# Weight differences ahead of their second parts, and four smaller changes of order, in a hybrid trunk kernel

## The chip, the cores and the metric

The kernel runs on one core of one Trainium2 chip. The metric is the device time of one execution in microseconds (us). In the profile TensorE is PE (its weight loads are PEld), VectorE is DVE, ScalarE is ACT, GpSimd is POOL and SyncE is SP. SP computes nothing; it issues transfers. An engine works through its instructions in program order, and so does a queue of transfers at its issuing end: an instruction that waits holds up all that stands behind it on that engine.

## The reference, cut to what matters

One layer of a streaming encoder over 2048 prompt frames and 32 sample frames of 1024 features, in float32.

```python
def layer(h, p, conv_hist, pool_hist, pos, g_mix, w_in, conv_w, conv_b, pool_w, pool_scale,
          w_out, g_ple, w_ple_gate, w_ple):
    hn = rmsnorm(h, g_mix)
    proj = hn @ w_in                                   # 1024 -> 3072
    hA, bA, cA, zA, vB, zB = jnp.split(proj, [W_A, 2 * W_A, 3 * W_A, 4 * W_A, 4 * W_A + W_B], axis=-1)
    yA, new_conv = short_conv_mixer(hA, bA, cA, zA, conv_hist, conv_w, conv_b)
    yB, new_pool = pooling_mixer(vB, zB, pool_hist, pos, pool_w, pool_scale)
    h = h + jnp.concatenate([yA, yB], axis=-1) @ w_out # 1024 -> 1024
    gate = jax.nn.sigmoid(rmsnorm(h, g_ple) @ w_ple_gate)
    h = h + (p @ w_ple) * gate                         # the embedding, 256 -> 1024
    return h, new_conv, new_pool
```

The first mixer is `b * conv3(c * h) * silu(z)`, a causal convolution of width 3 for each channel. The second takes trailing means over 2, 4, 8 and 16 frames less the frame itself, a 128x128 map for each group of channels, a scale, and times `silu(z)`. A last RMSNorm with `g_final` closes the trunk.

## The kernel before, in words

**Products in parts.** Every float32 operand of a matmul is held as two parts: a first part, cast to the type in which TensorE reads float32 at its full rate (a ScalarE copy, called cast in the profile), and a second part, the operand less the first (a VectorE subtraction). A product is then three matmuls for each 128 rows of the contraction: first by first, first by second, second by first (`FINE`, L100). `split` (L81 and L84) does this for frames and for the input projection's weights, `weight_part` (L195, L199, L202) for the weights of the later products.

**Seven products instead of eight.** Both operands are cut into 2 x 2 blocks and combined in the manner of Strassen. The weights come as 11, 21, 22 and the combinations T1 to T4 (one VectorE subtraction each, L195, which overwrites a block in place), the frames as 11, 12, 22 and S1 to S4. `seven` (L254) walks through the seven products with three PSUM banks X, Y, Z (x_o, y_o, z_o in the profile) and calls between them the functions that it is handed: `between` holds work to be issued after a product. `carry` and `out` take a finished bank to SBUF.

**Stages, in order of time.**

1. The input projection, up to about 536 us. Two groups of two tiles of 512 frames; for each of four channel blocks j three pairs of projections run, (zb, v), (c, h) and (za, b), each pair one `seven` of its own (`Unit`, L625 for its matmuls). With `both`, which is true for j = 0 of the second group only, the first two pairs run interleaved and the third follows. `pair_weights` prepares the weights of a pair; its `make(q)` makes the parts of one of them. `conv` (L1080) and `pool_sums`, `pool_split`, `mix` (L1062, L1072, L849 to L853) are the two mixers' own steps, placed between products by the table `mixes`. Beside the products of the first group, frames of the second are transposed on TensorE and combined (`four`, L465): a bank `pt_g` is taken, four transposes write it, VectorE or ScalarE reads it. `tbank` is a ring of two PSUM banks, `bank` one of six.
2. The embedding product (`embed`, L109) for the first seven tiles of 128 frames, 536 to 555 us. Its outputs lie in a space `eouts` and GpSimd's queue stores them (L168). The space belongs to a slot in which the weights 22 and T4 of the output product are put afterwards.
3. The output product with w_out, 555 to 726 us (`seven("o...")`, L185), pairs of tiles. T2 of its weights is made beside the last two embedding tiles; T3, then 21 and 22, then T4 beside the products of the first pair (`LATER`, where a number is the product behind which its function is called). `pin=True` keeps an instruction in the order in which it is written; the others may be put elsewhere by the scheduler. The lower rows of w_out, wo_b, are loaded on SP's queue, the last of them on GpSimd's.
4. The embedding for the remaining tiles, 726 to 754 us. Its weight wq is loaded on SP's queue (L1479) into a slot that the output product's last reads set free. The lower rows of the gate's weight, wg_b (L1363), and the frames' parts, pps (L129), are on the same queue.
5. The gate product, 754 to 930 us (`seven("g...")`), a loop over pairs of tiles, and a last pair with an order of its own (`last_pair`). For a pair the loop loads h and the embedding e (L377), and hn, the rows that are turned for the next pair; `gate_ops` adds to h (L1544), `done_g` squares, scales (GpSimd's ms_f and rstd_f, L73 and L77; VectorE's L1551) and stores (L1552, on GpSimd's queue). h's buffers are a ring, so that a load of h waits for the store of the tile that had the buffer before.

The weights' steps of the output product, cut from the code:

```python
        def third():
            hold.append(weight_parts(W, tops, bots, "T3", pin=True))

        def left():
            weight_parts(W, tops, bots, "21", pin=True)
            weight_slot(W, "wo", "22", "T4")
            hold.append(weight_parts(W, tops, bots, "22", pin=True))
            more(0)

        LATER = {1: third, 2: left, 3: later(1), 4: later("T4", 2)}
```

Of the kernel before, what the change touches and what calls it, by code (L numbers as in the profile page):

```python
# [9 lines left out]
F32 = mybir.dt.float32  # L10
F32R = mybir.dt.float32r
AF = mybir.ActivationFunctionType
ALU = mybir.AluOpType
# [16 lines left out]
NH = D // 2  # L30
KH = KC // 2
# [5 lines left out]
def trunk(ctx, tc, x_p, x_s, c_conv, c_pool, p_p, p_s, g_mix, w_in, conv_w, conv_b, pool_w,  # L37
          pool_scale, w_out, g_ple, w_gate, w_ple, g_fin, y_p, y_s, sc_p, sp_p, sc_s, sp_s):
    nc = tc.nc
# [6 lines left out]
    h_d = tc.dram_tile([T, D], F32, name="h_d")  # L46
# [140 lines left out]

    def weight_part(W, q, k, top, bot, ready=False, pin=False):

        b11, b12 = top[:, :NH], top[:, NH:]  # L190
        b21, b22 = (bot[:, :NH], bot[:, NH:]) if bot is not None else (None, None)
        t, x, y = {"11": (b11, None, None), "T1": (b11, b12, b11), "T2": (b11, b22, b11), "T3": (b12, b22, b12),
                   "22": (b22, None, None), "21": (b21, None, None), "T4": (b21, b21, b11)}[q]
        if x is not None and not ready:
            ins = nc.vector.tensor_tensor(t, x, y, op=ALU.subtract)  # L195
            if pin:
                tc.keep_in_program_order(ins)
        hi, lo = W[q][0][:, k], W[q][1][:, k]
        ins = nc.scalar.copy(hi, t)  # L199
        if pin:  # L200
            tc.keep_in_program_order(ins)
        return nc.vector.tensor_tensor(lo, t, hi.bitcast(F32), op=ALU.subtract)  # L202

    def weight_parts(W, tops, bots, *names, order=range(KH), pin=False):

        for q in names:
            for k in order:
                ins = weight_part(W, q, k, tops[k], bots[k] if bots else None, pin=pin)
        return ins
# [170 lines left out]
    with ExitStack() as s1:  # L380
# [20 lines left out]
        def put(piece, src, later=False):  # L401

            split(piece[:, :, 0], piece[:, :, 1], src, later=later)
# [56 lines left out]
        def turn(x, half, name, get=tbank, later=False):  # L460
            xt, n, _ = x
            pt = get(name)
            for k in range(KH):
                kk = half * KH + k
                ins = nc.tensor.transpose(pt[:, k * P:k * P + n], xt[:n, kk * P:(kk + 1) * P], ident[:n, :n])  # L465
                if later:
                    tc.keep_in_program_order(ins)
            return pt.rearrange("p (k t) -> p k t", k=KH)[:, :, :n]
# [5 lines left out]
        def four(xs, tag):  # L474

            for half in range(2):
                yield [turn(x, half, f"pt_{tag}_{i}_{half}", later=True) for i, x in enumerate(xs)]

# [99 lines left out]
        def pair_weights(gi, ka, kb, j, name, ring, s_ring, ring_b, pin):  # L578
# [31 lines left out]
            def make(q):  # L610
                if q == "S2":
                    sub(a11, s_t, a11)
                if q == "S4":
                    sub(a12, a12, a11)
                t = wtile(f"w_{name}_{q}")
                put(t, src[q])
                return t

# [52 lines left out]
        def in_turn(ins):  # L671
            tc.keep_in_program_order(ins)
# [142 lines left out]
        class Unit:  # L815
# [157 lines left out]
            def seven(self, B, aside, both=False):  # L973
# [20 lines left out]
                def h_first(ps):  # L994
                    mul(at(U, HU, 0), ps, self.cols(c_s, 0))
                    for b in range(2):
                        self.conv(b)

# [30 lines left out]

                def mix_and_split():  # L1030
                    self.mix(0)
                    self.pool_split(1)

                mixes = {(1, 2): first_mix, (1, 7): lambda: self.mix(1)}
                if both:
                    mixes = {(1, 7): lambda: self.pool_sums(1), (2, 2): mix_and_split, (2, 5): lambda: self.mix(1)}
                steps = [self.pair(*pairs[i], ring[i], ftile if both and i == 1 else None, both and i == 2) for i in range(3)]
# [239 lines left out]
    with ExitStack() as s2:  # L1277
# [142 lines left out]
        def third():  # L1420
            hold.append(weight_parts(W, tops, bots, "T3", pin=True))

# [52 lines left out]
        got = {0: load_pps(st.tile([P, 2, 2, P], F32R, tag="t", name=f"pps_{EARLY}"), EARLY, nc.sync)}  # L1475
        head, _ = rows_of_weight(cmb, "wg_b", g_d, 1, (0, 1))
        for k in range(2):
            for h in range(2):
                last_q = nc.sync.dma_start(wp[k][h].bitcast(F32), wl_d[k][h])  # L1479
        bots = head  # L1480
        with tc.issue_after(last_q.ins):
            bots += rows_of_weight(cmb, "wg_b", g_d, 1, (2, 3))[0]
        first_h = load_rows(xh, "hn", 0, h_d)
# [88 lines left out]
        def last_pair(i, A, before):  # L1572
# [9 lines left out]

            h = [load_rows(xh, "h", i + b, h_d) for b in range(2)]
            tt = nc.vector.tensor_tensor
# [167 lines left out]
        for k in range(KH):  # L1752
            weight_part(W, "T4", k, tops[k], bots[k], True)

# [12 lines left out]
        for i in range(0, NT - 3, 2):  # L1767
            A = S.pop(i)
            following = prep_g(i + 2, not i)
            h = [load_rows(xh, "h", i + b, h_d, queue=nc.sync if i else nc.gpsimd) for b in range(2)]  # L1770
            e = [load_rows(ya, "e", i + b, e_d) for b in range(2)]
            seven(f"g{i}", A, W, *gate_ops(h, e, P, f"g{i}", i), following)
            done_g(i, h[0])
            if i in (0, 2, 4):
                next(short_steps)
            if i + 2 < NT - 3:
                done_g(i + 1, h[1])
# [29 lines left out]
```

## Time and profile before

| what | us |
|---|---|
| median of 3 runs | 936.03 (935.65 to 938.8) |
| the profiled execution | 940.35 |
| its span | 938.3 |
| TensorE busy in the span | 909.1 |
| VectorE, ScalarE, GpSimd busy | 698.1, 459.0, 149.7 |
| mean granted TensorE clock | 0.991 of full speed |

The profile is of one execution. Its span runs from the first instruction to the last; the time of the execution includes what lies around it, 2.05 us here. A row of the timeline reads: start, duration, engine, line, operation, output and inputs by their names in the program, shape, count, and in brackets the idle time of the engine just before with what ended it. A row of the waits reads: who waited for whom, us in total, times, longest. A row of the windows gives the length of a stretch, busy us and instructions of each engine, the granted TensorE clock, the share of the transfer engines and the GB/s that they moved. A row of the transfers ends with the size and the us from issue to landing. In the chain that ended last each piece has a start and a length.

### The profile page before, as it was taken

Reading aid. Unit: us, or ns where it says so; the run is one execution under the profiler, and the core shown is the slowest. Engines: PE = TensorE matmul, PEld = TensorE weight load, DVE = VectorE, ACT = ScalarE, POOL = GpSimd, SP = SyncE. Lnnn points to the kernel's source line nnn. Section 1 sums busy time; section 2 is a strip of 40 time slices with the busy share of each in tenths; the row PEclk is TensorE's granted clock in tenths of the full one; section 3 lists DMA queues with packets and bytes.
Section 4 is the critical chain, followed back from the end, with each engine's and each line's share of the span. In section 5 each row is a group of like instructions: output and inputs, shape, how many; then the busy total and the mean of one; then the engine's idle time right before and its main releaser. Section 6 shows DMA issues by size and latency. Waiting matters only on the chain.

```text
span 938.3 us, 12210 instructions
## 1 busy us (share of the span) xinstructions
PE 909.1 (97%) x4186; PEld 727.1 (77%) x4186; DVE 698.1 (74%) x1148; ACT 459.0 (49%) x828; POOL 149.7 (16%) x295
## 2 busy tenths in 40 slices
PE   8999999999999999999999998999999999999996
PEld 6788887878888788766688885878787788778885
DVE  6895788797993787736668578765655988698884
ACT  7752544465453354523343375434434865456653
POOL 2200121222121032100010121112111211111112
PEclk9999999999999999999999998999999999999999
DMA  8165295747599674777753785776778776465653
GB/s 270 50 204 183 87 277 175 214 156 238 172 344 425 152 246 152 245 224 224 233 164 108 249 290 181 222 242 222 213 233 273 297 259 191 157 208 203 215 188 124
DMA packets 113243, 199.56 MB, mean 213 GB/s; under 512 B 13206, under 2 KB 69950, under 8 KB 112157
## 3 DMA queue, kind: packets, MB, share of 16 engines
q1 hardware_dynamic: 90749, 124.53, 42.3%
q0 software_dynamic: 19984, 69.87, 22.0%
q10 hardware_dynamic: 2448, 4.39, 1.3%
q8 instruction: 33, 0.54, 0.2%
q14 instruction: 29, 0.24, 0.1%
HBM read 133.06 MB, written 65.67 MB: 212 GB/s over the span
## 4 chain that ended last, share of the span: by engine, by line
PE 64%; DVE 5%; DMA 5%; ACT 2%; issue 2%; POOL 1%; POOLq 0%; SPq 0%; DVEq 0%; ACTq 0%
PE x_g L185 8%; PE x_zab L625 7%; PE x_o L185 6%; PE x_ch L625 6%; PE x_zbv L625 5%; PE e L109 4%; PE z_g L185 4%; PE z_zab L625 4%; PE z_ch L625 3%; PE z_o L185 3%; PE z_zbv L625 2%; PE y_g L185 2%; PE y_zab L625 1%; PE y_o L185 1%; PE new L1124 1%
## 5 line engine op out<-in xcount | busy, mean ns | idle before, releaser
L185 PE MATMUL x_o<-wo,y 128*128 128x512 f32 x192 | 48.3, 407 | 3.1 <-ACT wo L199 3.1
L185 PE MATMUL z_g<-wg,g_S 128*128 128x512 f32 x192 | 49.3, 401 | 0.0
L185 PE MATMUL x_o<-wo_T,y_S 128*128 128x512 f32 x192 | 47.5, 393 | 1.4 <-ACT wo_T L199 0.5
L185 PE MATMUL z_o<-wo,y_S 128*128 128x512 f32 x192 | 47.7, 390 | 0.5 <-ACT y_S L81 0.4
L185 PEld LDWEIGHTS x_o<-wo,y 128*128 128x128 f32 x192 | 38.0, 199 | 11.9 <-ACT wo L199 3.5
L185 PEld LDWEIGHTS x_o<-wo_T,y_S 128*128 128x128 f32 x192 | 35.6, 188 | 10.9 <-DVE c_o L1292 1.6
L625 PE MATMUL x_zab<-B,w_zab_S 128*128 128x512 f32 x168 | 41.1, 392 | 1.8 <-ACT w_zab_S L81 1.4
L185 PEld LDWEIGHTS z_o<-wo,y_S 128*128 128x128 f32 x192 | 35.9, 188 | 8.7 <-ACT y_S L81 0.8
L185 PEld LDWEIGHTS z_g<-wg,g_S 128*128 128x128 f32 x192 | 36.4, 193 | 7.6 <-ACT c_g L1532 0.2
L625 PE MATMUL z_zab<-B,w_zab_S 128*128 128x512 f32 x168 | 41.1, 392 | 0.8 <-ACT w_zab_S L81 0.8
L625 PE MATMUL x_ch<-B,w_ch_S 128*128 128x512 f32 x168 | 41.8, 392 | 0.0
L625 PE MATMUL z_ch<-B,w_ch_S 128*128 128x512 f32 x168 | 40.8, 391 | 1.0 <-ACT U L945 1.0
L625 PE MATMUL z_zbv<-B,w_zbv_S 128*128 128x512 f32 x168 | 40.7, 391 | 0.0
L625 PE MATMUL x_zbv<-B,w_zbv_S 128*128 128x512 f32 x168 | 40.6, 391 | 0.0
L625 PEld LDWEIGHTS x_zab<-B,w_zab_S 128*128 128x128 f32 x168 | 31.2, 188 | 9.8 <-ACT w_zab_S L81 1.8
L625 PEld LDWEIGHTS z_ch<-B,w_ch_S 128*128 128x128 f32 x168 | 31.3, 188 | 8.7 <-ACT U L945 1.4
L625 PEld LDWEIGHTS z_zab<-B,w_zab_S 128*128 128x128 f32 x168 | 31.2, 188 | 8.5 <-ACT w_zab_S L81 1.3
L625 PEld LDWEIGHTS x_zbv<-B,w_zbv_S 128*128 128x128 f32 x168 | 31.4, 188 | 7.3 <-issue 0.8
L625 PEld LDWEIGHTS x_ch<-B,w_ch_S 128*128 128x128 f32 x168 | 31.3, 188 | 7.3 <-issue 0.8
L625 PEld LDWEIGHTS z_zbv<-B,w_zbv_S 128*128 128x128 f32 x168 | 31.3, 188 | 7.2 <-issue 0.8
L81 ACT CAST y_S<-y_fS 128x512 fp32r<-128x512 f32 x28 | 17.0, 619 | 25.5 <-PE x_o L185 11.0
L1551 DVE SCALAR_TENSOR_TENSOR h<-h,rstd_f,g_bc 128x1024 f32<-128x1024 f32 (+1 forms) x15 | 19.2, 1280 | 12.7 <-POOL rstd_f L77 12.0
(561 smaller groups left out, 2295.4 us busy)
## 6 DMA issues: line engine op xcount, KB each, us to landing
wn<-in_w_in_dram SPq DMA_DIRECT2D x24, 512.0 KB, 3.9
p_dT<-T POOLq DMA_DIRECT2D x16, 512.0 KB, 5.4
y<-y_d SPq DMA_DIRECT2D x16, 512.0 KB, 4.0
e<-e_d SPq DMA_DIRECT2D x15, 512.0 KB, 5.0
x<-in_x_prompt_dram SPq DMA_DIRECT2D x14, 512.0 KB, 4.0
h<-h_d SPq DMA_DIRECT2D x14, 512.0 KB, 3.5
out_dram<-h POOLq DMA_DIRECT2D x14, 512.0 KB, 3.5
B<-p_d POOLq DMA_DIRECT2D x3, 2048.0 KB, 15.6
```

Of the source, the lines that this page charges most:

```text
L81: ins = nc.scalar.copy(hi, src)
L109: nc.tensor.matmul(ps, pps[:, a, k], wp[k][b][:, cs], start=k + q == 0, stop=k == 1 and q == 2)
L185: nc.tensor.matmul(ps[:n], lhs[:, k, a, :n], w[b][:, k], start=start and k + q == 0, stop=k == KH - 1 and q == 2, skip_group_check=True)
L625: nc.tensor.matmul(ps, lhs[:, k, x], b[:, k, y], start=start and k + q == 0, stop=stop and k == KH - 1 and q == 2, skip_group_check=True)
L1124: nc.tensor.matmul(ps[g * DEC:g * DEC + DEC, :NB // 2].rearrange("p (kind j c) -> p kind j c", kind=2, j=4), xs[:, k], t[:, g], start=k == ...
L1551: nc.vector.scalar_tensor_tensor(h[:n], h[:n], rf[:n], g_bc[:n], op0=ALU.mult, op1=ALU.mult)
```

## The change

It has five parts.

- A. `weight_part` becomes three functions: the source (with the difference, where there is one), the first part, the second part. `weight_parts` issues the differences of two k steps ahead: first part of k, difference of k + 2, second part of k. T3's differences of the output product go to GpSimd (`sums=nc.gpsimd`), and there they aren't pinned. With `pin` the second parts are pinned as well, which they weren't before.
- B. All four lower rows of the gate's weight are issued behind the four loads of wq; before, two of them stood ahead.
- C. The loads of h in the gate stage go to GpSimd's queue in every pair, the last included; before, only the first pair's did.
- D. In the input projection, where `both` is true: half of the convolution (`conv(1)`) and the second pooling sums move behind the second step of the third pair, `pool_split(1)` and `mix(1)` a product later than before. The difference for S2 of the third pair's weights is made, and pinned, right behind the parts of 11.
- E. Of the transposes in `four`, the second half's banks come from the ring of six instead of the ring of two.

```diff
                 nc.tensor.matmul(ps[:n], lhs[:, k, a, :n], w[b][:, k], start=start and k + q == 0,
                                  stop=k == KH - 1 and q == 2, skip_group_check=True)
 
-    def weight_part(W, q, k, top, bot, ready=False, pin=False):
+    def weight_source(W, q, k, top, bot, pin=False, sums=nc.vector):
 
         b11, b12 = top[:, :NH], top[:, NH:]
         b21, b22 = (bot[:, :NH], bot[:, NH:]) if bot is not None else (None, None)
         t, x, y = {"11": (b11, None, None), "T1": (b11, b12, b11), "T2": (b11, b22, b11), "T3": (b12, b22, b12),
                    "22": (b22, None, None), "21": (b21, None, None), "T4": (b21, b21, b11)}[q]
-        if x is not None and not ready:
-            ins = nc.vector.tensor_tensor(t, x, y, op=ALU.subtract)
-            if pin:
+        if x is not None:
+            ins = sums.tensor_tensor(t, x, y, op=ALU.subtract)
+            if pin and sums is nc.vector:
                 tc.keep_in_program_order(ins)
-        hi, lo = W[q][0][:, k], W[q][1][:, k]
-        ins = nc.scalar.copy(hi, t)
+        return t
+
+    def weight_first(W, part, q, pin=False):
+
+        k, t = part
+        ins = nc.scalar.copy(W[q][0][:, k], t)
         if pin:
             tc.keep_in_program_order(ins)
-        return nc.vector.tensor_tensor(lo, t, hi.bitcast(F32), op=ALU.subtract)
-
-    def weight_parts(W, tops, bots, *names, order=range(KH), pin=False):
+
+    def weight_second(W, part, q, pin=False):
+
+        k, t = part
+        ins = nc.vector.tensor_tensor(W[q][1][:, k], t, W[q][0][:, k].bitcast(F32), op=ALU.subtract)
+        if pin:
+            tc.keep_in_program_order(ins)
+        return ins
+
+    def weight_parts(W, tops, bots, *names, order=range(KH), pin=False, sums=nc.vector):
 
         for q in names:
-            for k in order:
-                ins = weight_part(W, q, k, tops[k], bots[k] if bots else None, pin=pin)
+            at = lambda k: (W, q, k, tops[k], bots[k] if bots else None)
+            todo = [(k, weight_source(*at(k), pin, sums)) for k in order[:2]]
+            for k in order[2:]:
+                weight_first(W, todo[0], q, pin)
+                following = (k, weight_source(*at(k), pin, sums))
+                weight_second(W, todo.pop(0), q, pin)
+                todo.append(following)
+            for part in todo:
+                weight_first(W, part, q, pin)
+                ins = weight_second(W, part, q, pin)
         return ins
 
     def frame_parts(cmb, tmp, name, a11, a12, a21, a22, *between):
...
         def four(xs, tag):
 
             for half in range(2):
-                yield [turn(x, half, f"pt_{tag}_{i}_{half}", later=True) for i, x in enumerate(xs)]
+                yield [turn(x, half, f"pt_{tag}_{i}_{half}", get=bank if half else tbank, later=True) for i, x in enumerate(xs)]
 
         def frame_sums(xs, tag, dst):
 
...
             src = {"11": a11, "12": a12, "S2": a11, "S1": s_t, "S3": s3, "S4": a12, "22": a22}
 
             def make(q):
-                if q == "S2":
+                if q == "S2" and not pin:
                     sub(a11, s_t, a11)
                 if q == "S4":
                     sub(a12, a12, a11)
                 t = wtile(f"w_{name}_{q}")
                 put(t, src[q])
+                if q == "11" and pin:
+                    in_turn(sub(a11, s_t, a11))
                 return t
 
             return make
...
 
                 def h_first(ps):
                     mul(at(U, HU, 0), ps, self.cols(c_s, 0))
-                    for b in range(2):
-                        self.conv(b)
+                    self.conv(0)
+                    if not both:
+                        self.conv(1)
 
 
                 za = [self.cols(V, b) for b in range(2)]
...
                     self.pool_block(1)
 
 
-                def mix_and_split():
+                def second_conv():
                     self.mix(0)
-                    self.pool_split(1)
+                    self.pool_sums(1)
+                    self.conv(1)
 
                 mixes = {(1, 2): first_mix, (1, 7): lambda: self.mix(1)}
                 if both:
-                    mixes = {(1, 7): lambda: self.pool_sums(1), (2, 2): mix_and_split, (2, 5): lambda: self.mix(1)}
+                    mixes = {(2, 2): second_conv, (2, 4): lambda: self.pool_split(1), (2, 6): lambda: self.mix(1)}
                 steps = [self.pair(*pairs[i], ring[i], ftile if both and i == 1 else None, both and i == 2) for i in range(3)]
 
                 def go(i, s):
...
             return run
 
         def third():
-            hold.append(weight_parts(W, tops, bots, "T3", pin=True))
+            hold.append(weight_parts(W, tops, bots, "T3", pin=True, sums=nc.gpsimd))
 
         def left():
             weight_parts(W, tops, bots, "21", pin=True)
...
         shared = slot("wq")
         wp = [[shared[:, (2 * k + h) * D:(2 * k + h + 1) * D] for h in range(2)] for k in range(2)]
         got = {0: load_pps(st.tile([P, 2, 2, P], F32R, tag="t", name=f"pps_{EARLY}"), EARLY, nc.sync)}
-        head, _ = rows_of_weight(cmb, "wg_b", g_d, 1, (0, 1))
         for k in range(2):
             for h in range(2):
                 last_q = nc.sync.dma_start(wp[k][h].bitcast(F32), wl_d[k][h])
-        bots = head
         with tc.issue_after(last_q.ins):
-            bots += rows_of_weight(cmb, "wg_b", g_d, 1, (2, 3))[0]
+            bots = rows_of_weight(cmb, "wg_b", g_d, 1)[0]
         first_h = load_rows(xh, "hn", 0, h_d)
 
         rest_e = [*range(EARLY, NT - 2), NT - 1]
...
             wp = []
             chunk = lambda: wp.extend(load_wp(cmb, "wl", nc.sync))
 
-            h = [load_rows(xh, "h", i + b, h_d) for b in range(2)]
+            h = [load_rows(xh, "h", i + b, h_d, queue=nc.gpsimd) for b in range(2)]
             tt = nc.vector.tensor_tensor
             carry, _ = gate_ops(h, [e], P, f"g{i}", i)
             hg = [ring4(ya, f"hg_{b}") for b in range(2)]
...
             nc.vector.tensor_tensor(bots[k][:, :NH], bots[k][:, :NH], tops[k][:, :NH], op=ALU.subtract)
         W["T4"] = halves(shared)[:2]
         for k in range(KH):
-            weight_part(W, "T4", k, tops[k], bots[k], True)
+            weight_first(W, (k, bots[k][:, :NH]), "T4")
+            weight_second(W, (k, bots[k][:, :NH]), "T4")
 
         def short_gate():
             n = tiles[NT - 1][1]
...
         for i in range(0, NT - 3, 2):
             A = S.pop(i)
             following = prep_g(i + 2, not i)
-            h = [load_rows(xh, "h", i + b, h_d, queue=nc.sync if i else nc.gpsimd) for b in range(2)]
+            h = [load_rows(xh, "h", i + b, h_d, queue=nc.gpsimd) for b in range(2)]
             e = [load_rows(ya, "e", i + b, e_d) for b in range(2)]
             seven(f"g{i}", A, W, *gate_ops(h, e, P, f"g{i}", i), following)
             done_g(i, h[0])
```

## The prediction, made before the changed kernel was run

> **What bounds the kernel now.** First the page: its head and the busy line.
>
> ```profile
> span 938.3 us, 12210 instructions
> PE 909.1 (97%) x4186; PEld 727.1 (77%) x4186; DVE 698.1 (74%) x1148; ACT 459.0 (49%) x828; POOL 149.7 (16%) x295
> ```
>
> TensorE is busy for 909.1 of 938.3 us. The edits neither add nor remove a matmul of it, so they can win only what it idles (29.2 us) and what its busy time is stretched by a lower clock. The view of waits says whom TensorE idles for:
>
> ```profile
> PE x_o L185 <- ACT wo L199: 3.1, 1, 3.1
> ...
> PE e L109 <- DMA wq<-wl_d: 2.0, 1, 2.0
> PE pth L1506 <- ACT ho L1504: 2.0, 1, 2.0
> ...
> PE x_zab L625 <- ACT w_zab_S L81: 1.4, 1, 1.4
> PE pt_g L465 <- DVE 11_1_0_1459 L84: 1.3, 1, 1.3
> ...
> PE z_zab L625 <- ACT w_zab_S L81: 0.8, 1, 0.8
> ...
> PE x_o L185 <- ACT wo_T L199: 0.5, 1, 0.5
> ```
>
> These seven are single events, and the edits lie at them. A table of windows around the four longest places (columns: length; PE, weight loads, VectorE, ScalarE, GpSimd busy; PE clock; DMA share; GB/s) shows a second cost:
>
> ```profile
> 574.50:577.60 3.10, 0.04 (x1) 0.00 (x0) 3.10 (x7) 1.28 (x3) 0.00 (x0) 0.90 0.91 321
> 577.60:583.20 5.60, 5.54 (x13) 4.41 (x14) 2.95 (x6) 1.15 (x2) 2.19 (x4) 0.50 0.80 218
> 727.20:729.20 2.00, 0.04 (x1) 0.04 (x1) 2.00 (x3) 1.47 (x2) 0.61 (x1) 1.00 1.00 394
> 730.20:733.90 3.70, 3.70 (x15) 3.18 (x14) 3.70 (x7) 3.56 (x8) 2.64 (x5) 0.55 1.03 399
> 810.10:812.10 2.00, 0.00 (x1) 0.00 (x0) 0.12 (x1) 0.67 (x2) 0.00 (x0) 1.00 0.15 57
> 812.50:815.50 3.00, 3.00 (x12) 2.53 (x11) 2.27 (x4) 2.10 (x5) 0.00 (x0) 0.50 0.78 231
> 153.50:154.80 1.30, 0.01 (x1) 0.00 (x0) 1.30 (x4) 1.30 (x3) 0.00 (x0) 1.00 0.00 0
> 154.80:160.00 5.20, 5.19 (x25) 4.40 (x26) 4.33 (x8) 1.87 (x4) 1.75 (x2) 1.00 0.84 214
> ```
>
> After idles of 3.1, 2.0 and 2.0 us the granted clock falls to about half; after 1.3 us it does not. Length times lost share of the clock prices it: 5.6 x 0.50 = 2.8, 3.7 x 0.45 = 1.7, 3.0 x 0.50 = 1.5 us. So the three long waits cost 5.9, 3.7 and 3.5 us.
>
> **Part A, weights of the output product (T2, T3 and the block behind them).** VectorE's differences, in the timeline of the old order:
>
> ```profile
> 554.63 0.69 DVE L195 TENSOR_TENSOR wo_t<-wo_b,wo_t 128x512 f32<-128x512 f32 x1
> 556.01 0.69 DVE L202 TENSOR_TENSOR wo_T<-wo_t,wo_T 128x512 fp32r<-128x512 f32 x1 [0.69 <-ACT wo_T L199]
> ```
>
> Difference, cast and second part follow each other, so each of the eight k steps of T2 and T3 stands 0.69 us for the cast. With differences two ahead these stands vanish for T2, and T3's four differences leave VectorE for GpSimd. All of T3, 21 and 22 now forms one pinned block, twelve casts, on ScalarE; y_12's cast, which stood between such casts, comes behind it, and in TensorE's order two products of 21 with y_12 stand ahead of S3 with T3. So the old wait at 574.5 goes (T4, whose differences come behind, is ready about 573 by a hand chain of 0.5 per cast and 0.7 per VectorE step, an estimate), and y_12 becomes what is late. When? The casts of 22 overwrite the slot that holds the embedding's outputs, so they wait for those stores, which GpSimd issues:
>
> ```profile
> 556.75 0.53 POOL L168 DMA_DIRECT2D e_d<-eouts  x1 [2.50 <-ACT eouts L167]
> ...
> e_d<-eouts POOLq DMA_DIRECT2D x1, 512.0 KB, 4.7
> ...
> e_d<-eouts POOLq DMA_DIRECT2D x1, 512.0 KB, 7.6
> ...
> L1605 POOL TENSOR_TENSOR hg<-h,g_bc 128x512 f32<-128x512 f32 x1 | 1.3, 1297 | 0.1
> ```
>
> The last store issues at 556.75 and lands after 4.7 us. In the new order of GpSimd's queue the four differences stand between the stores. The one difference-like operation of GpSimd on two such tiles took 1.30 us; four are 5.2, of which by my hand chain 1.5 falls ahead of the last store (the rest lies in the 2.50 us that GpSimd sat before it, and that between the earlier ones). Store at 558.25, landed 562.95, four casts of 22 behind it:
>
> ```profile
> 566.63 4.26 ACT L199 CAST wo<-wo_b 128x512 fp32r<-128x512 f32 x8
> ...
> 563.52 1.75 PE L185 MATMUL x_o<-wo_T,y_S 128*128 128x512 f32 x7
> ```
>
> 4.26 / 8 = 0.53 each, so 565.1, and y_12's cast one more, 565.7. TensorE reaches this place at 563.52: a new idle of 2.2 us, and by the rows after 2.0 us a half clock worth 1.7. Gain: 3.1 + 2.8 + the 0.5 us that T3's cast costs TensorE, less 2.2 and 1.7: **2.5 us**. Bounds: at best no new wait, 6.4. At worst GpSimd's differences take twice 1.30 or hold the queue, the last store lands at 566 and the idle is 4.7 with 2.8 of clock: 6.4 - 7.5 = -1.1. I take the middle because 1.30 was measured on this very form.
>
> The Trainium skill ("TensorE: Matmul & The Clock Gate", Part 1: The HAM clock gate) says that the clock falls after at least one idle window of about 3.4 us. The rows above differ: 2.0 us was enough, twice, so the measurement decides here; by the page the new idle would cost 1.7 us less and the sum would be that much larger. The Trainium skill ("SBUF — State Buffer", SBUF: two separate sides) speaks against part A: a VectorE operation on two SBUF inputs and a GpSimd operation lock each other out of a shared port pair. No row of before isolates this; it is what would make the lower bound.
>
> **Part B, gate rows behind the embedding weight.** SP's queue and the chain that ended last:
>
> ```profile
> 717.96 2.50 SPq L1479 DMA_DIRECT2D wq<-wl_d  x4
> ...
> 713.63 6.49 DMA wg_b<-g_d
> ...
> 720.14 8.98 DMA wq<-wl_d
> ...
> 725.92 1.24 PE L109 MATMUL e<-wq,pps 128*128 128x512 f32 x4
> ```
>
> The last wq row landed at 729.12 because wg_b's row of 713.63 was still moving until 720.12. Now the four wq loads (2 MB) go first, still not before 717.96, when the slot comes free. At the 394 GB/s of the window 727.20 they take 5.3 us: 724.5 or so, ahead of 725.92. So 3.7 us go. What is late next: the wg_b rows land some 5 us later each, but they feed the gate product, which comes behind the whole embedding; behind them in the queue stands the next pps block, which took 9.5 us:
>
> ```profile
> pps<-pp_d SPq DMA_DIRECT2D x1, 256.0 KB, 9.5
> ```
>
> Issued at 722.79, it landed at 732.3. Now four wg_b rows (2 MB, 5.3 us) lie between 724.5 and it: about 730 to 732, while TensorE, no longer delayed, reaches that block about 730.1 (725.92, then twelve products and eight transposes at the 0.21 us of the window 154.80). An idle of 0 to 2 us; I subtract 1.0: **2.7 us**, bounds 3.7 and -0.5 (2.5 idle with 1.7 of clock).
>
> **Part C, h loads on GpSimd's queue.** SP's queue again, then the chain:
>
> ```profile
> 796.87 1.75 SPq L1515 DMA_DIRECT2D hn<-h_d  x4
> 804.30 0.34 SPq L377 DMA_DIRECT2D h<-h_d  x1
> 804.68 0.43 SPq L377 DMA_DIRECT2D hn<-h_d  x1
> ...
> 801.29 2.96 DMA out_dram<-h
> ...
> 804.68 6.73 DMA hn<-h_d
> ```
>
> The h load waited for the store that frees its buffer (801.29 + 2.96), and hn stood behind it. Without it hn issues at about 798.7 and, at the same 6.73, lands at 805.4; its transposes' turn is 810.1. The idle of 2.0 and its 1.5 of clock go: **3.5 us**, bounds 3.0 (a little of the wait is ScalarE's own copy) and 4.2. The h load now issues about 805.1 on GpSimd. Behind it there stand the next ms_f and rstd, and these have cover:
>
> ```profile
> 824.23 0.18 POOL L73 TENSOR_SCALAR ms_f<-ssq_f 128x1 f32<-128x1 f32 x1 [19.20 <-ACT junk L94]
> 815.63 0.68 DVE L1544 TENSOR_TENSOR h<-h,e 128x512 f32<-128x512 f32 x1
> ```
>
> GpSimd sat idle 19.20 us, and the freshly loaded h may be wanted as early as 815.63, so 10.5 us after the issue. The other moved loads are covered likewise.
>
> **Parts D and E, the input projection.** D moves one difference ahead of the convolution and half of the convolution, with the pooling split and the mix, a product later, in the first block of the second group of tiles, the one with its first two pairs interleaved.
>
> ```profile
> 320.09 2.73 DVE L1080 SCALAR_TENSOR_TENSOR c_s<-U,vec,c_s 128x512 f32<-128x512 f32 x4
> 323.35 0.68 DVE L587 TENSOR_TENSOR raw_zab_0a<-s_zab,raw_zab_0a 128x512 f32<-128x512 f32 x1
> 324.73 0.74 PE L625 MATMUL x_zab<-B,w_zab_S 128*128 128x512 f32 x2 [1.35 <-ACT w_zab_S L81]
> ```
>
> The difference now runs ahead of the 2.73 us of convolution, so at about 320 and over 3 us earlier; its cast then ends before 323.4 (324.73 - 1.35), when TensorE comes for it. The 1.35 and 0.83 us of TensorE's idle go: **2.2 us**, bounds 0.5 (the second parts still meet the mixes' casts) and 2.8. E lets every second transpose take a bank of the other ring; the 1.3 us wait of pt_g for a bank's reader goes: **1.3**, bounds 0.6 and 1.6.
>
> **Sum.** 2.5 + 2.7 + 3.5 + 2.2 + 1.3 = 12.2 us. The profiled execution took 940.35 us, 4.3 above the median of 936.03, so it would come to 928.15, and on the median's footing to **923.8 us**. All upper ends: 6.4 + 3.7 + 4.2 + 2.8 + 1.6 = 18.7, so 917.3. All lower ends: -1.1 - 0.5 + 3.0 + 0.5 + 0.6 = 2.5, so 933.5.
>
> **Rivals.** (1) GpSimd and VectorE lock each other in part A, its end -1.1: sum 8.6, 927.4 us. For it: GpSimd sits between stores that the casts of 22 wait for. Against it: the 1.30 us row. (2) The pps block takes wq's place as the wait, B at -0.5: sum 9.0, 927.0 us. For it: 9.5 us of landing; against: twelve products and transposes come first. (3) The idles only move: each product that starts earlier meets the next supplier's lateness; A and B give nothing, C to E half: about 3.5, 932.5 us, or, if less is left, no change: this is the case in which the change does not do what it says. (4) Slower, by GpSimd's queue in the gate stage: in each of the six loops of pairs an h load stands in order behind a store and lands more than 10.5 us after its issue. VectorE then stops in order at the addition to h, and no product's bank comes free. Six idles of 2.0 us with 1.5 of clock are 21.0; less A, B, D and E (8.7) the time is 948.3 us. It needs three such loops to eat the gain. Against it: h lands in 3.5 us on SP; for it: the store of e whose row stands under part A with 7.6 us, issued on GpSimd near 547.6 with another close to it.
>
> **How the numbers follow.** Forecast 0.60, rival (1) 0.10, (2) 0.08, (3) 0.08, (4) 0.14. The predicted time is the forecast's, 923.8. The range 916 to 934 takes in the two sums of bounds and rivals (1) to (3) but for the part of (3) that is no change; outside lies (4) and that part, together 0.2. A run of this kernel tells 0.3% (2.8 us) from no change. Faster: 0.60 + 0.10 + 0.08 + 0.02 = 0.80; the same 0.06, the rest of (3); slower 0.14.
>
> **What would show it.** A: the wait of x_o for wo at 574 is gone, one of y_o for y_12 (about 2 us) stands near 563, and GpSimd's four differences are 1.3 us each; 2.6 would speak for rival (1). B: e's wait for wq is gone; a wait of e for pps in its place is rival (2). C: pth's wait for ho near 810 is gone, and clock 1.00 stands there; VectorE waiting for h loads is rival (4). D and E: x_zab's and pt_g's waits are gone. It would be wrong as a whole if TensorE's idle sum stayed at some 29 us.

## The result, and the profile after

The changed kernel takes 930.23 us (median of 5 runs, 928.67 to 931.26) against 936.03 us (median of 5, 935.09 to 938.8): a ratio of 0.9934, 95% interval 0.9915 to 0.9954. That is 5.8 us or 0.66% faster. The prediction, 923.8 us in a range of 916 to 934, had the sign and the range right and the gain, 12.2 us, twice too large.

The page of the changed kernel, head and busy line:

```profile
span 928.4 us, 12196 instructions
PE 902.4 (97%) x4186; PEld 724.1 (78%) x4186; DVE 699.7 (75%) x1144; ACT 458.8 (49%) x828; POOL 164.5 (18%) x313
```

TensorE is busy for 6.7 us less with the same 4186 matmuls. Most of that is clock: while it works, the granted clock falls behind one wait in this profile and behind three in the one before. It idles 26.0 us instead of 29.2. Its waits:

```profile
PE e L109 <- DMA pps<-pp_d: 3.2, 1, 3.2
...
PE y_o L185 <- ACT y L81: 2.3, 1, 2.3
...
PE x_o L185 <- ACT c_o L1320: 1.3, 1, 1.3
...
PE x_o L185 <- DVE x L1315: 0.9, 1, 0.9
...
PE x_g L185 <- DVE c_g L1561: 0.6, 1, 0.6
...
PE pth L1527 <- ACT ho L1525: 0.5, 1, 0.5
```

All seven waits that the prediction shows are gone, but for 0.5 us of pth's and 0.2 us that x_zab still waits, now for the second part of its weights. New ones stand near them: y_o for y_12's cast at 561.65, as forecast (2.3 us against 2.2), and e for a pps block at 720.8, where the forecast had 1.0 us and there are 3.2. The windows around the two (length; PE, weight loads, VectorE, ScalarE, GpSimd busy; PE clock; DMA share; GB/s):

```profile
561.65:564.00 2.35, 0.01 (x2) 0.01 (x1) 2.35 (x5) 2.35 (x6) 0.00 (x0) 1.00 0.00 0
564.00:566.00 2.00, 2.00 (x9) 1.55 (x10) 2.00 (x5) 1.96 (x4) 0.00 (x0) 1.00 0.01 4
...
720.80:724.00 3.20, 0.02 (x1) 0.00 (x0) 3.14 (x6) 2.83 (x6) 2.20 (x4) 0.98 0.83 282
724.00:726.00 2.00, 1.97 (x5) 1.59 (x6) 2.00 (x5) 2.00 (x5) 0.61 (x1) 0.50 1.03 413
726.00:728.00 2.00, 2.00 (x8) 1.57 (x7) 2.00 (x4) 2.00 (x5) 0.00 (x0) 0.67 1.02 418
```

After y_12's wait the clock stays at 1.00; after the wait for pps it falls, which costs 2.0 x 0.50 + 2.0 x 0.33 = 1.7 us.

The spans of the two profiled executions differ by 9.9 us, the medians by 5.8. The profiled execution of before took 940.35 us, longer than any of the five that are timed. So the first experiment runs the kernel before again.

### The profile page after: what moved, and what is told of

The parts are those of the page before. It is cut to its first block, busy times and chain, and to the rows that moved or that the text cites. A ratio compares the mean times of both kernels' runs of the same rounds, so it can differ in the third digit from the quotient of the medians.

```text
span 928.4 us, 12196 instructions
## 1 busy us (share of the span) xinstructions
PE 902.4 (97%) x4186; PEld 724.1 (78%) x4186; DVE 699.7 (75%) x1144; ACT 458.8 (49%) x828; POOL 164.5 (18%) x313
## 5 line engine op out<-in xcount | busy, mean ns | idle before, releaser
L185 PE MATMUL z_g<-wg,g_S 128*128 128x512 f32 x192 | 47.3, 392 | 0.0
L185 PE MATMUL x_o<-wo,y 128*128 128x512 f32 x192 | 45.5, 390 | 0.9 <-DVE x L1315 0.9
L185 PEld LDWEIGHTS x_o<-wo,y 128*128 128x128 f32 x192 | 36.0, 188 | 8.9 <-DVE x L1315 1.3
```

What stands on the lines that cost most here:

```text
L185: nc.tensor.matmul(ps[:n], lhs[:, k, a, :n], w[b][:, k], start=start and k + q == 0, stop=k == KH - 1 and q == 2, skip_group_check=True)
```

## The experiments

The experiments ran in three sets of four kernels, each set on one chip beside the kernel before. The sets' medians of the kernel before are 937.23, 937.57 and 936.8 us.

### The kernel before, again (first set)

No edit.

> The kernel before, unchanged, to see how its executions differ. Theory 1 (the half clock after an idle of 2 to 3 us falls in some executions only, and the profiled one of 940.35 us had three of them, 6.0 us): the mean clock of its runs lies between 0.991 and 0.997, the higher the shorter the run, and a second profile lacks at least one of the three half-clock stretches (near 577, 730, 812). Theory 2 (half clock in every execution): 0.991 in all runs and all three stretches again; then the change's gain of 5.8 between the medians was lost in a place that the profiles do not show.

Measured: 939.06 us (12 executions, 933.43 to 942.57), ratio to the kernel before 1.0011, interval 0.9991 to 1.0032. Over the three sets 61 executions of this kernel lie between 933.43 and 942.57 us, with a mean clock from 0.990 (942.25, 942.53) to 0.997. Its second profile, of the execution of 933.43 us, has these waits:

```profile
PE x_o L185 <- ACT wo L199: 3.1, 1, 3.1
...
PE pth L1506 <- ACT ho L1504: 2.0, 1, 2.0
...
PE e L109 <- DMA pps<-pp_d: 0.6, 1, 0.6
```

and these windows, at the place of the first and behind that of the second:

```profile
577.60:583.20 5.60, 5.60 (x19) 4.54 (x20) 4.03 (x8) 1.72 (x3) 2.19 (x4) 0.75 0.75 209
...
808.00:812.00 4.00, 4.00 (x20) 3.31 (x19) 4.00 (x7) 2.03 (x4) 0.00 (x0) 1.00 0.69 219
```

The four longest waits that ScalarE ends have the same length to 0.1 us in both profiles; a short one, z_o for y_S, has 0.4 and 0.8. What follows the two at which the edits lie differs: 5.6 x 0.25 = 1.4 us of clock instead of 2.8 after the first (1.7 instead of 3.4, if one counts from 576 to 586, where the clock is back), nothing instead of 1.5 after the second. And e's wait for wq, 2.0 us in the first profile, isn't there; a wait of 0.6 us for pps is. Theory 1 holds. The slope to the clock is loose (938.63 us at 0.996, 938.52 at 0.991), so something else carries part of the spread. In the two profiles it is in part the waits for transfers; the other executions have no profile that could show it.

### Part B undone (first and third set)

```diff
+        head, _ = rows_of_weight(cmb, "wg_b", g_d, 1, (0, 1))
         for k in range(2):
             for h in range(2):
                 last_q = nc.sync.dma_start(wp[k][h].bitcast(F32), wl_d[k][h])
+        bots = head
         with tc.issue_after(last_q.ins):
-            bots = rows_of_weight(cmb, "wg_b", g_d, 1)[0]
+            bots += rows_of_weight(cmb, "wg_b", g_d, 1, (2, 3))[0]
```

> The changed kernel with part B undone (two gate rows ahead of wq again). Theory 1 (B moved the wait from wq to pps and made it longer, 3.2 us with 1.7 of clock instead of 2.0 with 0 to 1.7): TensorE's wait for pps is gone, that for wq is back with about 2.0 us, and the time is 0 to 2 us below the changed kernel's 930.23, so about 929. Rival (B as I forecast it, worth 2.7 us): about 933. Second rival (pps is late for its buffers, not for the rows ahead of it): the wait for pps stays.

Measured: 928.69 us (4 executions, 926.93 to 929.22), ratio to the kernel before 0.9904 (0.9886 to 0.9921). The profile has no wait for wq, and 1.2 us for pps; theory 1 had expected the wait for wq back and the one for pps gone. Since the changed kernel did not run in that set, both ran once more side by side:

> Part B undone, a second time, now beside the changed kernel on one chip. Theory (behind wq, all four gate rows stand before the pps blocks, 2 MB instead of 1 MB, and the wait for wq that B was to remove is not in every execution): 1 to 3 us below the changed kernel of this call, with the wait for pps at 0.5 to 1.5 us, no wait for wq over 0.5 us, and clock 1.00 between 720 and 735. Rival (the 1.5 us between the two in the earlier calls came from the chip): within 0.7 us of it.

> The changed kernel beside it: 929 to 932.5, the wait for pps 2 to 4.5 us with a half clock behind it.

Measured: 929.48 us (5 executions), ratio 0.9911 (0.9894 to 0.9927), against 931.32 us (5), 0.9933 (0.992 to 0.9946), for the changed kernel: 1.8 us faster without part B. The two intervals overlap a little; the first set, where the kernel without B lies 1.5 us below the changed kernel's first median, points the same way. In the changed kernel's profile of this set e waits 2.3 us for pps, and the clock stays at 1.00 behind it, where a half clock was expected; behind y_o's wait it falls. Waits of the kernel without B in this set, then SP's queue in the timelines of the changed kernel's first profile and of this one:

```profile
PE e L109 <- DMA wq<-wl_d: 0.8, 1, 0.8
...
PE e L109 <- DMA pps<-pp_d: 0.3, 1, 0.3
```

```profile
709.09 1.76 SPq L1501 DMA_DIRECT2D wq<-wl_d  x4
710.90 1.89 SPq L1386 DMA_DIRECT2D wg_b<-g_d  x4
713.29 23.81 SPq L129 DMA_DIRECT2D pps<-pp_d  x8
```

```profile
700.66 0.38 SPq L1386 DMA_DIRECT2D wg_b<-g_d  x1
...
704.28 0.48 SPq L1386 DMA_DIRECT2D wg_b<-g_d  x1
...
709.58 1.76 SPq L1502 DMA_DIRECT2D wq<-wl_d  x4
711.39 0.90 SPq L1386 DMA_DIRECT2D wg_b<-g_d  x2
713.22 20.95 SPq L129 DMA_DIRECT2D pps<-pp_d  x8
```

wq issues at the same time in both (709.1 and 709.6), when its slot comes free. Without B two rows of 512 KB move before that, and 1 MB stands between wq and the pps blocks; with B it is 2 MB. At the 413 GB/s of the window 724.00 the difference is 2.5 us, which fits what is lost. My bound of 0.5 us on the wait for wq was passed by 0.3, and the 0.3 us for pps lie below the 0.5 to 1.5 that I had put.

### Pps blocks ahead of the gate rows (first set)

```diff
         with tc.issue_after(last_q.ins):
+            for c in (1, 2):
+                got[c] = load_pps(st.tile([P, 2, 2, P], F32R, tag="t", name=f"pps_{EARLY + c}"), EARLY + c, nc.sync)
             bots = rows_of_weight(cmb, "wg_b", g_d, 1)[0]
```

> The changed kernel with the second and third pps block loaded right behind wq, ahead of the four gate rows. Theory 1 (the pps block is late because 2 MB of gate rows stand ahead of it): TensorE's wait for pps (3.2 us, 1.7 of clock behind it) is gone, under 0.5 us is left, and the time is 3 to 5 us below 930.23, about 926. Rival (its buffer is what it waits for): the wait stays and the gate rows are later too, 930 or more.

Measured: 931.08 us (6 executions, 927.35 to 932.82), 0.993 (0.991 to 0.9949): no better than the changed kernel. SP's queue and the wait:

```profile
709.53 1.76 SPq L1501 DMA_DIRECT2D wq<-wl_d  x4
715.07 2.72 SPq L129 DMA_DIRECT2D pps<-pp_d  x2
717.84 2.31 SPq L1386 DMA_DIRECT2D wg_b<-g_d  x4
720.48 6.22 SPq L129 DMA_DIRECT2D pps<-pp_d  x4
```

```profile
PE e L109 <- DMA pps<-pp_d: 3.3, 1, 3.3
```

The rival is right: the queue stops from 711.3 to 715.07 at the first pps load, whose buffer is one of the ring that the output product's carries use. The two blocks come in time, but the four rows now issue 7 us later and the next block stands behind them. The 2 MB have only moved.

### y_12's cast earlier (first set)

The casts of 22 move behind the second product; y_12's parts come before them, and the copies of x_o and z_o are pinned.

```diff
             weight_parts(W, tops, bots, "21", pin=True)
+            tc.keep_in_program_order(more(0))
+
+        def rest_left():
             weight_slot(W, "wo", "22", "T4")
             hold.append(weight_parts(W, tops, bots, "22", pin=True))
-            more(0)
+            more(1)
...
-        LATER = {1: third, 2: left, 3: later(1), 4: later("T4", 2)}
+        LATER = {1: third, 2: left, 3: rest_left, 4: later("T4", 2)}
```

> The changed kernel with y_12's cast and the copy of x_o (c_o) put ahead of the four casts of 22, which move behind them. Theory 1 (the twelve casts in one block make y_12 late): TensorE's wait of y_o for y (2.3 us) falls under 0.9 us and the time by about 1.5 us to 928.7. Rival (T3's weights are what is late next): a wait of x_o for wo_T takes its place, and the time stays at 930.

Measured: 932.43 us (6 executions), 0.9945 (0.9924 to 0.9965). The cast was what y_o waited for, since its wait falls to 0.3 us; the time did not fall. Waits, then windows, of this kernel:

```profile
PE x_o L185 <- DVE x L1315: 3.0, 1, 3.0
...
PE y_o L185 <- ACT y L81: 0.3, 1, 0.3
```

```profile
570.00:572.00 2.00, 0.08 (x1) 0.00 (x0) 2.00 (x4) 0.00 (x0) 0.00 (x0) 1.00 0.95 352
572.00:574.00 2.00, 0.88 (x4) 0.77 (x5) 2.00 (x4) 0.00 (x0) 1.33 (x2) 1.00 1.08 365
574.00:576.00 2.00, 2.00 (x8) 1.53 (x7) 1.98 (x4) 1.15 (x2) 0.11 (x1) 0.62 1.01 214
```

VectorE has no pause in these windows, and the last product of the pair waits for its addition on x_o. The rival that a later wait takes the place holds, though not at T3's weights where I had put it. In this stretch VectorE, not ScalarE, is the engine that TensorE waits for. Another part of the time lies elsewhere: e waits 4.5 us for pps in this profile, against 2.3 to 3.2 in the changed kernel's three.

### Part A undone (second set), and T3 alone on VectorE

```diff
         for q in names:
-            at = lambda k: (W, q, k, tops[k], bots[k] if bots else None)
...
+            for k in order:
+                part = (k, weight_source(W, q, k, tops[k], bots[k] if bots else None, pin, sums))
+                weight_first(W, part, q, pin)
+                ins = weight_second(W, part, q)
...
-            hold.append(weight_parts(W, tops, bots, "T3", pin=True, sums=nc.gpsimd))
+            hold.append(weight_parts(W, tops, bots, "T3", pin=True))
```

The second kernel has the last two lines alone. Beside them the changed kernel ran again.

> The changed kernel once more, so that the other three stand beside it on one chip. Theory (the time left over the forecast lies in the wait for pps, 3.2 us and its clock, and in the spread of both kernels): 928 to 933, median near 930.5, clock 0.993 to 0.997; its profile shows the wait of e for pps at 2 to 5 us again, the wait of y_o for y at 2.3 us, and after the latter a half clock in some executions and not in others. Rival (the pps wait of the first profile was chance): under 1 us.

> The changed kernel with part A undone: differences in step with casts and second parts, T3's on VectorE, second parts not pinned. Theory (A took 3.1 + 0.5 of waits, and the clock behind them in some executions, and put 2.3 + 1.3 + 0.9 in their place, in the trace 3.6 us earlier at the second pair): 1 to 4 us above the changed kernel, so 931 to 934, with the wait of x_o for wo back at about 3.1 us. Rival (A only moved its wait): within 1 us of the changed kernel.

> The changed kernel with T3's four differences on VectorE, all else of the new order kept. Theory (each difference on GpSimd stops VectorE for its 1.3 us: two operations of 1.28 together took 4.21, one of 0.69 took 1.92; but VectorE waits there for the last row of w_out anyway, so the stops cost nothing, and behind them it is saved four differences of 0.6): VectorE's operations between 544 and 555 all take 0.7 again, and the time is 1 to 2.4 us above the changed kernel, 931 to 933. Rival (the stops are on the path that sets T2): 1 to 3 us below it, 927 to 929.

Measured: the changed kernel 931.52 us (6 executions, 929.49 to 932.80), 0.9923 (0.9902 to 0.9945), its wait for pps 2.3 us and that of y_o 2.4. A undone 933.77 us (12), 0.9966 (0.9948 to 0.9984): 2.3 us slower. T3 on VectorE 931.04 us (6), 0.9924 (0.99 to 0.9948): the same as the changed kernel.

A undone brings the old wait back (row of the waits), and here no fall of the clock follows it (window behind it):

```profile
PE x_o L185 <- ACT wo L203: 3.1, 1, 3.1
```

```profile
573.50:579.00 5.50, 5.21 (x22) 3.97 (x22) 5.04 (x9) 2.72 (x6) 2.31 (x5) 1.00 0.85 245
```

The profiles of A undone and of the changed kernel beside it start the output product at the same time (551.48 and 551.47 us), and A undone reaches the second embedding 2.6 us later (719.63 against 717.02). TensorE's idle time in between explains 0.8 us of this (5.4 against 4.5). The other 1.8 us count as busy time for the same 705 matmuls at a clock of 1.00: short stalls between single matmuls that stand in no row of the waits. From 559.64 to 564.68, for example, A undone has 13 matmuls, where 12 in a row take 2.7 us.

What GpSimd's differences do to VectorE stands in the changed kernel's first profile, VectorE first, then GpSimd:

```profile
544.92 4.21 DVE L84 TENSOR_TENSOR y_S<-y,y_S 128x512 fp32r<-128x512 f32 x2 [0.23 <-ACT y_S L81]
...
552.56 1.92 DVE L210 TENSOR_TENSOR wo_T<-wo_t,wo_T 128x512 fp32r<-128x512 f32 x1
```

```profile
545.25 1.31 POOL L195 TENSOR_TENSOR wo_t<-wo_b,wo_t 128x512 f32<-128x512 f32 x1
...
547.27 1.30 POOL L195 TENSOR_TENSOR wo_t<-wo_b,wo_t 128x512 f32<-128x512 f32 x1
...
552.62 1.30 POOL L195 TENSOR_TENSOR wo_t<-wo_b,wo_t 128x512 f32<-128x512 f32 x1
```

and with T3 on VectorE the same two groups read:

```profile
545.82 1.29 DVE L84 TENSOR_TENSOR y_S<-y,y_S 128x512 fp32r<-128x512 f32 x2 [0.22 <-ACT y_S L81]
...
549.76 0.68 DVE L210 TENSOR_TENSOR wo_T<-wo_t,wo_T 128x512 fp32r<-128x512 f32 x1
```

Each difference on GpSimd stops VectorE for about its own length (4.21 - 1.29 = 2.9 for two, 1.92 - 0.68 = 1.2 for one), so moving them there frees no VectorE time: a difference costs VectorE itself about 0.6 us. The theory's reason that the stops cost nothing does not hold either. In the changed kernel VectorE reaches the last difference of T2 at 554.40 without any wait; with T3 on VectorE it does so at 551.21, after 0.77 us of waiting for the last row of w_out. What it wins there it then spends on T3's own differences. Both theories named these stops; neither's time came out. The kernel loses the wait of 2.4 us at y_12's cast and the 1.1 us of x_o for its copy (c_o), gets one of 2.0 us for the next such copy, and stays where it is. Part A's gain thus comes from the differences two ahead and the pinned order, not from GpSimd; which of the two it is was not tried.

### Part C undone (second set)

```diff
-            h = [load_rows(xh, "h", i + b, h_d, queue=nc.gpsimd) for b in range(2)]
+            h = [load_rows(xh, "h", i + b, h_d, queue=nc.sync if i else nc.gpsimd) for b in range(2)]
```

and the default queue in the last pair.

> The changed kernel with part C undone: h on SP's queue again. Theory (hn behind h in SP's queue cost the 2.0 us wait of pth, and a clock of 1.5 in some executions): 2.0 to 3.5 us above the changed kernel, 932 to 934, the wait of pth for ho back at about 2 us. Rival (GpSimd's queue costs elsewhere in the gate stage what it saves here): within 1 us of the changed kernel.

Measured: 930.35 us (6 executions, 929.27 to 934.01), 0.9918 (0.9894 to 0.9941): the same as the changed kernel, by the rival. The wait is back (row of the waits), and the clock behind it holds (window):

```profile
PE pth L1527 <- ACT ho L1525: 1.8, 1, 1.8
```

```profile
804.50:808.00 3.50, 3.50 (x19) 2.95 (x20) 2.37 (x4) 2.50 (x5) 0.00 (x0) 1.00 0.84 246
```

The changed kernel's first profile has 0.5 and 0.6 us at pth and x_g in its place; here x_g waits 0.3. That leaves 1.8 + 0.3 - 1.1 = 1.0 us of TensorE's idle for part C at this place. The end of the kernel takes it back: from TensorE's last matmul to the end of the span it is 9.2 to 9.6 us in the eleven profiles of kernels with part C, and 8.1 to 8.2 in the three without it (both of the kernel before, and this one: 928.8 against 920.64). So the rival is right, and the place is the end. The last store issues 3.2 us after the last matmul with and without part C (922.36 against 919.16, 923.84 against 920.64), so the difference lies behind that issue, 6.0 us to the end of the span against 5.0. What makes it longer no view shows. What the two small waits come from was not tried.

### Parts D and E undone (third set)

The hunks at `make`, `h_first`, `mixes` and `four` of the diff, reversed.

> The changed kernel with parts D and E undone. Theory (my forecast of 2.2 + 1.3; in the first traces the output product starts 3.6 us earlier): 3 to 4 us above the changed kernel of this call, so 934, with the waits of x_zab and z_zab for w_zab_S (1.4 and 0.8) and of pt_g (1.3) back. Rival (the output product's start is held by the last row of w_out anyway, so that the time won is lost there): 0 to 1.5 us above, with the wait of x_o for c_o at 557 gone.

Measured: 936.97 us (11 executions, 934.30 to 938.39), 0.9996 (0.9981 to 1.0012): 5.7 us above the changed kernel, more than expected. Its waits:

```profile
PE x_zab L644 <- ACT w_zab_S L81: 1.4, 1, 1.4
...
PE pt_g L484 <- DVE 11_1_0_1459 L84: 1.3, 1, 1.3
...
PE x_zbv L644 <- DVE V L967: 1.0, 1, 1.0
...
PE z_zab L644 <- ACT w_zab_S L81: 0.8, 1, 0.8
```

The three waits of the forecast are back with their 3.5 us. The other 0.8 that x_zbv waits beyond the changed kernel's 0.2 are new. Between 150 and 340 us TensorE idles 6.9 us here and 2.3 in the changed kernel's profile of this set, and the output product starts 4.9 us later (557.05 against 552.12), so most of the 5.7 arises in the input projection and is not lost at the output product's start, as the rival would have it.

### Two gate rows early, two behind three pps blocks (third set)

Part B undone, and ahead of the last two rows:

```diff
+        with tc.issue_after(last_q.ins):
+            for c in (1, 2, 3):
+                got[c] = load_pps(st.tile([P, 2, 2, P], F32R, tag="t", name=f"pps_{EARLY + c}"), EARLY + c, nc.sync)
```

> The changed kernel with two gate rows ahead of wq as before, and the other two behind three pps blocks. Theory (what stands ahead of the pps blocks makes them late): the wait for pps falls under 0.5 us and the time is 1 to 1.5 us below the kernel with B undone alone, near 927.5. Rival (the queue stops at the pps loads for their buffers, and the rows or a later block are late instead): a wait of 1 to 3 us at a later pps block or at the gate product's T2, and 929 or more.

Measured: 928.87 us (4 executions, 928.68 to 929.23), 0.9908 (0.9894 to 0.9922). No wait for pps is left, and 0.5 us for wq. The step from B undone alone, 0.6 us, is within the noise. It stands below both kernels: 7.9 us under the kernel before, 2.5 under the changed one, with intervals that just touch (0.9922 and 0.992). pth waits 1.9 us in two places here, 0.5 in the changed kernel.

## Why the prediction was right in sign and half wrong in size

By the paired medians the parts are worth: D and E 5.7 us, A 2.3, C -1.2 (no difference that the runs can tell), B -1.8. They add up to 5.0, near the 5.8 of the whole. That the time came out inside 916 to 934 is in part luck: B and C, 6.2 of the 12.2 us, gave nothing, and D and E gave more than their 3.5.

**Idle time.** Of the 12.2 us, 7.9 were idle time of TensorE and 4.3 clock. Its idle time fell by 3.1 us, from 28.6 in the mean of the two profiles of the kernel before to 25.5 in the mean of the changed kernel's three. By stage it fell by 3.6 us in the input projection, 150 to 340 us (D and E, forecast 3.5), and by 0.6 at the first pair of the output product, 520 to 600 (A, forecast 3.1 + 0.5 - 2.2 = 1.4). It rose by 1.5 between 700 and 760 (B, forecast a fall of 1.0). In the gate stage it fell by 1.4 between 760 and 850 and rose by 1.2 behind that (C, forecast a fall of 2.0).

**Half clock.** This is the other part of the sum that failed. I priced each wait with the clock that followed it in one profile, 2.8 + 1.7 + 1.5 us, and took 1.7 off for the new wait: 4.3 of the 12.2 us. The 61 executions of the kernel before have a mean clock of 0.9937 and the 16 of the changed one 0.9943; the shares lost are 5.9 and 5.3 us of their times, so the change won about 0.6 us of clock. This is rough: the means take in the stretch behind the last matmul, where 1.5 to 3.4 us are lost in these five profiles without a cost. Why the clock that I priced did not come is seen in the nine profiles that have y_o's wait of 2.3 to 2.4 us. In six of them the window 563 to 573 has a clock of 0.83, a loss of 1.7 us, just the forecast's figure, as here in the changed kernel's third profile; in three it is 1.00, as in its first:

```profile
563.00:573.00 10.00, 8.84 (x33) 7.21 (x34) 9.44 (x17) 5.93 (x12) 0.00 (x0) 0.83 0.51 174
```

```profile
563.00:573.00 10.00, 8.94 (x38) 6.98 (x38) 10.00 (x17) 5.76 (x11) 0.00 (x0) 1.00 0.53 177
```

So a wait of 2 to 3 us carries the loss with a chance, and the right price is loss times chance on both sides of the change. I had the warning in hand, a profiled execution 4.3 us above the median, and used it only to shift the total. The Trainium skill ("TensorE: Matmul & The Clock Gate", Part 1: The HAM clock gate) says that the window in which idle time is counted runs freely, so that the moment of a change varies. The spread here agrees with that. Its figure of one idle window of about 3.4 us does not: of the four waits of 2.0 us that these profiles have, three were enough (two in the first profile of before, one with T3 on VectorE), and 3.1 us without a fall occurred as well (A undone).

**Part B** was forecast at +2.7 us and is -1.8. Two steps failed. The wait for wq that it was to remove is 2.0 us in one profile, 0 in the second of the kernel before, 0 and 0.8 in the two without B. And the wait for pps, which I had seen and allowed 1.0 us for, is 3.2, 2.3 and 2.3 us in the three profiles of the changed kernel. Rival (2) describes it; its bound of 2.5 us of idle was the better value.

**Part C** was forecast at 3.5. The mechanism was right at the place it named: hn no longer stands behind h, and the 2.0 us there went. Its 1.5 of clock was not in two of the three profiles with the wait, 1.1 us of small waits stand in its place in the new order, and the end of the kernel is 1.1 us longer. The forecast had no term for these. Rival (4) did not occur: GpSimd's queue does wait for stores of the output, up to 3.3 us, but VectorE has no wait for a load of h.

**Part A** was forecast at 2.5 and measured at 2.3; y_12's wait was forecast at 2.2 us and is 2.3. Both agreements owe much to luck. The new order has two more waits, 1.3 us for c_o and 0.9 for x, that the forecast left out, so that by the waits alone nothing is won (3.1 + 0.5 against 2.3 + 1.3 + 0.9); the gain lies to a large part in the short stalls that no row of the waits has. The hand chain had the wrong cause for its start, since the stores of the embedding's outputs did not hold the casts of 22: the eight casts of 21 and 22 ran without a gap. The 1.3 us per difference on GpSimd held. Rival (1) describes what the trace shows, VectorE stopped by GpSimd, but not its price: without the stops the kernel is no faster. The Trainium skill ("SBUF — State Buffer", SBUF: two separate sides) has the lock, and the trace agrees with the times of both engines above. It did not decide the time.

**Parts D and E** were forecast at 3.5 us. In the first profiles of the two kernels the output product starts 555.36 - 551.74 = 3.6 us earlier; the undoing costs 5.7, so they are worth at least what was forecast. By the profiles this is the one term whose mechanism and size both came as forecast; why the undoing costs 2 us more is shown only in part.

## What to carry to other kernels

Profile the kernel before more than once before pricing its waits: here the long waits that a neighbouring engine ended had the same length in both profiles of the kernel before, while the wait that a transfer ended, and the clock behind either, had not. A queue's order decides which transfer is late: in three orders of the same loads, what was moved out of one wait came up as another. What helped was to issue two rows in an earlier and emptier stretch (256 GB/s from 700 to 709 us of the changed kernel's first profile, 345 from 709 to 725). Work given to GpSimd is not free for VectorE: four differences there stopped VectorE for longer than they take on it. And look at the end of the kernel too: a gain inside a stage can be lost behind the last matmul.

## What the runs showed of the hardware

A GpSimd subtraction of two 128x512 float32 tiles takes 1.30 us (three of four; the fourth took 1.70), and a VectorE subtraction beside it is longer by 1.2 to 1.5 us. TensorE's clock fell by half behind y_o's idle of 2.3 to 2.4 us in six of nine profiles and not in the other three, at the same place in nearly the same program. Each fall while TensorE worked cost 1.7 us of clock, or twice that, in the fourteen profiles. Identical programs spread by 1% (933.43 to 942.57 us).
